# FFN gate and up of 18 tiles as seven half-size products per pair of tiles, with three low parts made by an adding DMA

## The chip, the cores and the metric

The kernel runs on one core of a Trainium2 chip. The metric is the device time in microseconds of one execution; three executions of the kernel before took 1146.77, 1148.54 and 1149.83 us (median 1148.54).

## The reference

One layer of a hybrid decoder is applied to 512 prompt tokens and 8 x 8 sample tokens, 576 columns in all, with D_MODEL = 1024 and D_FF = 2816, in float32. The mixer in front (three recurrent branches and `w_out`) is not touched. The part that is touched is the SwiGLU:

```python
hf = rmsnorm(x, p["norm_pre_ffn"][l])
f = (jax.nn.silu(hf @ p["ffn_w_gate"][l]) * (hf @ p["ffn_w_up"][l])) @ p["ffn_w_down"][l]
x = x + rmsnorm(f, p["norm_post_ffn"][l])
```

## The kernel before

Activations lie transposed: 128 rows of a feature tile on the partitions, 576 tokens along the row, treated as two halves of 288. D_MODEL is 8 such tiles (`KT`), D_FF is 22 (`FT`).

Each float32 operand is split into a high part in float32r and a low part, the rest. A product of 128x128 weights with 288 columns is then three matmuls: high by high, high by low, low by high (lines 202 to 204). Activations are split once (`split`, lines 239 and 240). Weights arrive as 512 KB (`raw`, 128 x 8 x 128) by a DMA that SyncE issues, and `wsplit` cuts each into two parts of 4 x 128 = 512 columns: ScalarE copies the high part (L184), VectorE subtracts for the low part (L185). Both stand under a high priority for the planner.

The order of the instructions on each engine is not written by hand. The framework plans it with a timeline simulation, by priority and readiness, and the engines then run their queues in that order, waiting on semaphores. `issue_after` (from `behind(marks, ...)`) holds chosen matmuls behind small norm matmuls.

The FFN begins after `w_out` and two norms (lines 1290 to 1310), which are worked half by half; `xr` holds the normed activations in float32 and `hf[k]` their high and low parts. FFN gate and up of the first four tiles (`NG`) run half by half, in the order `HB`, with their weights kept split in the pool `wq` (12 buffers of high and low) and, for tile 0, in `wp` (4 buffers). So half 0 of these tiles can cover the norm of half 1.

The other 18 tiles come in a loop: `mm3(ff_load(...), hf)` gives gate and up, 48 matmuls each, into PSUM (six banks); `glu` applies tanh and two VectorE steps per half; `act_split` splits the result into `fh` and `fl`. After every fourth tile `down` multiplies four finished tiles with `w_down` (8 output tiles x 2 halves x 12 matmuls, line 1374, `product`) and adds into `xr` (L1399; L1397 copies the first time). `down(FT - 6, 2)` and a last block of four tiles follow, then the final norm and the stores. Raw weights use four buffers, two in `wp` and two in `sx`; split weights of the loop use 16: three of four allocations go to `wq`, one to `wp`.

Of the kernel before, what the change touches and what calls it, by code (L numbers as in the profile page):

```python
# [8 lines left out]
F32 = mybir.dt.float32  # L9
# [3 lines left out]
OP = mybir.AluOpType  # L13
# [52 lines left out]
def hybrid_step(ctx: ExitStack, tc: tile.TileContext, i, o, dbg=None):  # L66
# [13 lines left out]
    def nm(s):  # L80
        cnt[0] += 1
        return f"{s}_{cnt[0]}"
# [93 lines left out]
    def wsplit(raw, alloc=None, eng=None):  # L176
        c = raw.shape[1]
        if alloc:
            hi, lo = alloc(c)
        else:  # L180
            hi = wp.tile([128, c, 128], F32R, name=nm("wh"), tag="wh")
            lo = wp.tile([128, c, 128], F32R, name=nm("wl"), tag="wl")
        with tc.high_priority(offset=HIPRI):
            S.activation(hi, raw, AF.Copy)  # L184
            (eng or lo_eng()).tensor_tensor(lo, raw, hi.bitcast(F32), op=OP.subtract)  # L185
        return hi, lo, c

    def mmp(name="mm"):
        return psm[0].tile([128, 512], F32, name=nm(name), tag="mm")[:, 0:NH]
# [17 lines left out]
    def behind(marks, pos, t, n=KT):  # L207
        out = {}
        for k in range(n):
            for ins, p in zip(marks, pos):  # L210
                if p <= t * n + k:
                    out[k] = ins
        return out

    def mm_half(ws, x, half, after=None):
        acc, k0 = mmp(), 0
        for w in ws:
            mm_part(acc, w, k0, len(x), x, half, after)
            k0 += w[2]
        return acc  # L220
# [49 lines left out]
    def hsl(half):  # L270
        return slice(NH * half, NH * half + NH)
# [998 lines left out]
    def two(pool, tag_h, tag_l, **kw):  # L1270
        return lambda c: (pool.tile([128, c, 128], F32R, name=nm("wh"), tag=tag_h, **kw),
                          pool.tile([128, c, 128], F32R, name=nm("wl"), tag=tag_l, **kw))
# [38 lines left out]
    mix.close()  # L1311


    tp2 = ctx.enter_context(tc.tile_pool(name="tp2", bufs=1, reuse_waits="tile"))
    ar = ctx.enter_context(tc.tile_pool(name="ar", bufs=4, reuse_waits="tile"))
    wq = ctx.enter_context(tc.tile_pool(name="wq", bufs=4 * NG - 4, reuse_waits="tile"))
    sx = ctx.enter_context(tc.tile_pool(name="sx", bufs=2, reuse_waits="tile"))
    fp = ctx.enter_context(tc.tile_pool(name="fp", bufs=7, reuse_waits="tile"))
    mx = xr
    acts, fs_ = {}, {}  # L1320

    def act(m):
        if m not in acts:
            acts[m] = ar.tile([128, NT], F32, name=nm("ar"), tag="ar")
        return acts[m]

    def glu(t, pg, pu):
        S.activation(t, pg, AF.Tanh, scale=0.5)
        V.scalar_tensor_tensor(t, t, 1.0, pg, op0=OP.add, op1=OP.mult)
        V.tensor_tensor(t, t, pu, op=OP.mult)  # L1330

    def act_split(m):
        fs_[m] = split(act(m), fp.tile([128, NT], F32R, name=nm("fh"), tag="fh"),
                       fp.tile([128, NT], F32R, name=nm("fl"), tag="fl"))

    wqn = [0]

    def ff_alloc(c):
        wqn[0] += 1
        return two(wq, "qh", "ql")(c) if wqn[0] % 4 else two(wp, "wh", "wl")(c)  # L1340

    rawn = [0]

    def ff_raw():
        rawn[0] += 1
        return (wp if rawn[0] % 2 else sx).tile([128, KT, 128], F32, name=nm("wr"), tag="wr", bufs=2)

    def ff_load(src, alloc=None):
        raw = ff_raw()
        SY.dma_start(raw, src)  # L1350
        return [wsplit(raw[:, a:a + KC, :], alloc or ff_alloc, eng=V) for a in range(0, KT, KC)]

    wg = []
    for m in range(NG):
        al = two(wq, "qh", "ql") if m else two(wp, "wh", "wl")
        wg.append([ff_load(i[w][m], al) for w in ("w_gate", "w_up")])
    for m in range(NG):
        act(m)
    for half in range(2):
        for j, m in enumerate(HB[half]):  # L1360
            glu(act(m)[:, hsl(half)],
                *[mm_half(w, hf, half, None if half else behind(marks, (11, 24, 54, 62), 2 * j + a))
                  for a, w in enumerate(wg[m])])
            if half:
                act_split(m)


    def down_w(m, k0, n):
# [1 line left out]
        SY.dma_start(raw.rearrange("p (m k) c -> p m k c", m=2),  # L1370
                     i["w_down"][m:m + 2, :, k0:k0 + n, :].rearrange("m p k c -> p m k c"))
        return raw

    def product(w, k0, x):
        hi, lo, _ = w
        acc = mmp()
        for k, (xh, xl) in enumerate(x):
            PE.matmul(acc, hi[:, k0 + k, :], xh, start=k == 0, stop=False)  # L1378
            PE.matmul(acc, hi[:, k0 + k, :], xl, start=False, stop=False)  # L1379
            PE.matmul(acc, lo[:, k0 + k, :], xh, start=False, stop=k == len(x) - 1)  # L1380
        return acc

    def down(k0, n):
        for m in range(0, KT, 2):
# [13 lines left out]
                    else:  # L1398
                        V.tensor_tensor(xv, xv, ps, op=OP.add)  # L1399

    for m in range(NG, FT):
        pg, pu = (mm3(ff_load(i[w][m]), hf) for w in ("w_gate", "w_up"))
        for half in range(2):
            glu(act(m)[:, hsl(half)], pg[half], pu[half])
        act_split(m)
        if m % 4 == 1 and m < FT - 1:
            down(m - 5, 4)
    down(FT - 6, 2)

    nl_w = [0]  # L1410
# [172 lines left out]
```

## Time and profile before

| | |
|---|---|
| Runs | 1146.77, 1148.54, 1149.83 us |
| Profiled execution | 1148.92 us, its span 1147.1 us |
| Mean granted TensorE clock | 0.973 of 2.4 GHz |
| Busy: PE, VectorE, ScalarE, GpSimd | 1072.0, 747.6, 405.2, 301.5 us |
| DMA | 98.60 MB, on the queue that SyncE feeds but for instruction fetches |
| FFN from the end of the norms to the last block | about 735 to 1117 us |

Times of the profile count from the first instruction of the span. PE is TensorE's matmul, PEld its weight load, DVE is VectorE, ACT is ScalarE, POOL is GpSimd, SP or SPq is SyncE's queue. A line "A <- B" in waits says that A stood idle until B released it. Matmuls overlap in the pipeline, so the mean duration of one is longer than the step from one to the next; the step is the time of a stretch divided by its matmuls.

### The profile page before, as it was taken

To read this page: it belongs to the slowest core of one execution; us is meant where nothing else is said; L and a number is where in the kernel's file an instruction comes from. 1 tells how busy PE (TensorE), PEld (TensorE's weight loads), DVE (VectorE), ACT (ScalarE), POOL (GpSimd) and SP (SyncE) were. 2 spreads that over 40 slices of the span, in tenths; PEclk is the share of its full clock that TensorE was granted. 3 is DMA by queue.
4 is the path that set the end of the run, shared out by engine and by line. 5 is a ranking of instruction groups with operands and counts; after the bars stand their busy time and mean duration, and the time that the engine had idled before them with its cause. 6 is when DMAs were issued, how large, how long until landed. Compare 5 with 4: busy or idle time off the path is not lost.

```text
span 1147.1 us, 20072 instructions
## 1 busy us (share of the span) xinstructions
PE 1072.0 (93%) x7874; PEld 1023.4 (89%) x7874; DVE 747.6 (65%) x1642; ACT 405.2 (35%) x807; POOL 301.5 (26%) x372
## 2 busy tenths in 40 slices
PE   6997887998988999999999898999999999999994
PEld 5896877988878988998899898999999999999994
DVE  8989999987897779744646658653344444443346
ACT  4255753334532442322333435343322322322210
POOL 6477664435462225221002332000000000000014
PEclk8999998998999999999999998999999999999997
DMA  5322213233223143312113613042222232213002
GB/s 193 109 86 71 78 43 90 70 100 117 88 63 103 48 134 101 81 51 102 56 52 101 214 66 134 22 154 83 86 81 84 82 87 80 89 59 93 1 2 83
DMA packets 61235, 98.60 MB, mean 86 GB/s; under 512 B 26059, under 2 KB 34387, under 8 KB 61139
## 3 DMA queue, kind: packets, MB, share of 16 engines
q1 hardware_dynamic: 61138, 97.31, 27.4%
q8 instruction: 62, 1.02, 0.4%
q14 instruction: 35, 0.28, 0.1%
HBM read 89.05 MB, written 8.24 MB: 85 GB/s over the span
## 4 chain that ended last, share of the span: by engine, by line
PE 66%; DVE 22%; DMA 4%; issue 3%; ACT 2%; POOL 2%; SPq 0%; DVEq 0%; ACTq 0%
PE mm L202 15%; PE mm L203 15%; PE mm L204 15%; PE mm L1380 4%; PE mm L1378 4%; PE mm L1379 4%; DVE wl L185 3%; DVE cv L423 2%; PE up L1182 1%; DVE bu L1052 1%; DMA bc<-in_s_bc 1%; PE rows L265 1%; PE zq L1164 1%; DVE h L377 1%; DVE brl L240 1%
## 5 line engine op out<-in xcount | busy, mean ns | idle before, releaser
L184 ACT ACTIVATE wh<-wr 128x512 fp32r<-128x512 f32 x268 | 166.2, 629 | 369.2 <-PE mm L203 221.4
L185 DVE TENSOR_TENSOR wl<-wr,wh 128x512 fp32r<-128x512 f32 x248 | 186.7, 758 | 161.4 <-ACT wh L184 154.0
L202 PE MATMUL mm<-hh,wh 128*128 128x288 f32 x768 | 236.4, 308 | 13.2 <-ACT pad L410 5.3
L204 PE MATMUL mm<-hh,wl 128*128 128x288 f32 x768 | 233.9, 305 | 0.0
L203 PE MATMUL mm<-hl,wh 128*128 128x288 f32 x768 | 233.8, 305 | 0.0
L203 PE MATMUL mm<-hfl,wh 128*128 128x288 f32 x704 | 208.1, 296 | 1.7 <-DVE hfl L240 1.7
L204 PE MATMUL mm<-hfh,wl 128*128 128x288 f32 x704 | 207.9, 296 | 0.0
L202 PE MATMUL mm<-hfh,wh 128*128 128x288 f32 x704 | 207.8, 296 | 0.0
L202 PEld LDWEIGHTS mm<-hh,wh 128*128 128x128 f32 x768 | 148.7, 194 | 20.4 <-issue 6.6
L203 PEld LDWEIGHTS mm<-hl,wh 128*128 128x128 f32 x768 | 148.5, 193 | 3.7 <-issue 3.1
L204 PEld LDWEIGHTS mm<-hh,wl 128*128 128x128 f32 x768 | 148.1, 193 | 2.2 <-issue 1.5
L203 PEld LDWEIGHTS mm<-hfl,wh 128*128 128x128 f32 x704 | 133.0, 189 | 2.0 <-DVE hfl L240 2.0
L202 PEld LDWEIGHTS mm<-hfh,wh 128*128 128x128 f32 x704 | 133.4, 190 | 0.0
L204 PEld LDWEIGHTS mm<-hfh,wl 128*128 128x128 f32 x704 | 133.2, 189 | 0.0
L1436 POOL TENSOR_TENSOR fs<-fs,fs 128x288 f32<-128x288 f32 x9 | 7.3, 807 | 399.3 <-ACT fs L1432 399.3
L1380 PE MATMUL mm<-fh,wl 128*128 128x288 f32 x352 | 103.9, 295 | 0.0
L1378 PE MATMUL mm<-fh,wh 128*128 128x288 f32 x320 | 94.4, 295 | 0.0
L1379 PE MATMUL mm<-fl,wh 128*128 128x288 f32 x320 | 94.3, 295 | 0.0
L202 PE MATMUL mm<-brh,wh 128*128 128x288 f32 x224 | 68.1, 305 | 8.5 <-DVE mg L801 5.9
L203 PE MATMUL mm<-brl,wh 128*128 128x288 f32 x224 | 67.9, 303 | 1.8 <-DVE brl L240 1.2
L204 PE MATMUL mm<-brh,wl 128*128 128x288 f32 x224 | 67.5, 302 | 0.0
L1380 PEld LDWEIGHTS mm<-fh,wl 128*128 128x128 f32 x352 | 66.1, 188 | 0.0
(477 smaller groups left out, 2055.9 us busy)
## 6 DMA issues: line engine op xcount, KB each, us to landing
wr<-in_w_in SPq DMA_DIRECT2D x48, 512.0 KB, 3.6
wr<-in_w_gate SPq DMA_DIRECT2D x22, 512.0 KB, 3.6
wr<-in_w_up SPq DMA_DIRECT2D x22, 512.0 KB, 3.6
wr<-in_w_down SPq DMA_DIRECT2D x20, 512.0 KB, 3.6
wr<-in_w_out SPq DMA_DIRECT2D x8, 512.0 KB, 3.6
xa<-in_x SPq DMA_DIRECT2D x8, 288.0 KB, 5.9
xr<-in_x SPq DMA_DIRECT2D x4, 576.0 KB, 7.4
out_y<-xr SPq DMA_DIRECT2D x16, 144.0 KB, 1.8
```

Source lines behind the costliest of these rows:

```text
L184: S.activation(hi, raw, AF.Copy)
L185: (eng or lo_eng()).tensor_tensor(lo, raw, hi.bitcast(F32), op=OP.subtract)
L202: PE.matmul(acc, hi[:, k, :], xh[:, sl], start=k0 + k == 0, stop=False)
L203: PE.matmul(acc, hi[:, k, :], xl[:, sl], start=False, stop=False)
L204: PE.matmul(acc, lo[:, k, :], xh[:, sl], start=False, stop=k0 + k == n - 1)
L240: V.tensor_tensor(lo, x, hi.bitcast(F32), op=OP.subtract)
L265: m0 = PE.matmul(rows[:, 96 * b:96 * b + 96], rc[:96, b:b + 1].to_broadcast([96, 128]), ident[:96, :96], start=True, stop=True).ins
L377: (G if half and k % 4 == 3 else V).tensor_tensor(t, xa[:, k, hsl(half)], rw_[half], op=OP.mult)
L423: V.scalar_tensor_tensor(y[:, :CW], pad[:, k:k + CW], w[k], y[:, :CW], op0=OP.mult, op1=OP.add)
L1378: PE.matmul(acc, hi[:, k0 + k, :], xh, start=k == 0, stop=False)
L1379: PE.matmul(acc, hi[:, k0 + k, :], xl, start=False, stop=False)
L1380: PE.matmul(acc, lo[:, k0 + k, :], xh, start=False, stop=k == len(x) - 1)
```

## The change

The 18 tiles are taken in nine pairs m, m + 1. For gate, and again for up, the 256 x 1024 weights of a pair and the 1024 x 576 activations are read as 2 x 2 blocks: weights a11, a12, a21, a22 of 128 x 512 (tile by half of the features), activations by half of the features and half of the tokens. The four blocks of the result are formed by Winograd's scheme of seven products instead of eight.

- `hf_sums` forms the activation side once, on VectorE, in place in `xr`: t1, t2, t3 and t4, four subtractions of 1152 columns. t1 and t2 are split into a new pool `st`, t3 into `sx`, t4 over `hf[0..3]` of half 1.
- `pair_w` loads both raw weights (two DMAs of 512 KB) and forms s1, a21, a11, a12 by four additions of 512 columns on VectorE. Four of the seven weights (w2, w3, w4, w5) are split as before by ScalarE and VectorE.
- `wsplit_dma` splits the other three, w0 = a11, w1 = a12, w6 = a22: ScalarE copies the high part, ScalarE writes its negative to the low part's buffer, and a DMA issued by GpSimd adds the raw weights from HBM onto that (256 KB each).
- `pair` runs the products in the order w0, w2, w3, w4, w1, w5, w6, 12 matmuls each. Three sums are formed in PSUM: w1 continues the bank of w0 (`px`), w5 that of w3 (`pz`), w6 that of w4 (`pw_`), after ScalarE or VectorE has read the bank. ScalarE copies px to u; VectorE makes u + w2's product, c22 = u + pz, c22 + pw, c12 = u + pz, c21 = u + pw.
- The GLU is cut into `glu_g`, applied when gate's block is done, and `glu_u`. Tile m is worked in halves, tile m + 1 in one piece of 576. `down` of four tiles now runs between gate and up of every second pair (m = 4, 8, 12, 16).
- Pools: the first four tiles use `wload`, with the two raw buffers of `wp`. `wq` is opened after `fp`, so its tiles lie elsewhere, and closed after the first four tiles; `sx` opens in its place. The seven-product loop and `down` have six buffers for split weights, four in `wp` and two in `sx`. `fp` has six buffers instead of seven, `ar` two of double size.

```diff
--- before.py
+++ after.py
@@ -1311,58 +1311,157 @@
     mix.close()
 
 
     tp2 = ctx.enter_context(tc.tile_pool(name="tp2", bufs=1, reuse_waits="tile"))
-    ar = ctx.enter_context(tc.tile_pool(name="ar", bufs=4, reuse_waits="tile"))
-    wq = ctx.enter_context(tc.tile_pool(name="wq", bufs=4 * NG - 4, reuse_waits="tile"))
-    sx = ctx.enter_context(tc.tile_pool(name="sx", bufs=2, reuse_waits="tile"))
-    fp = ctx.enter_context(tc.tile_pool(name="fp", bufs=7, reuse_waits="tile"))
-    mx = xr
+    ar = ctx.enter_context(tc.tile_pool(name="ar", bufs=2, reuse_waits="tile"))
+    fp = ctx.enter_context(tc.tile_pool(name="fp", bufs=6, reuse_waits="tile"))
+    st = ctx.enter_context(tc.tile_pool(name="st", bufs=1, side="right", reuse_waits="tile"))
+    wqx = ExitStack()
+    wq = wqx.enter_context(tc.tile_pool(name="wq", bufs=4 * NG - 4, reuse_waits="tile"))
     acts, fs_ = {}, {}
 
+    def hquad(a, b):
+        return [(hf[4 * a + k][0][:, hsl(b)], hf[4 * a + k][1][:, hsl(b)]) for k in range(4)]
+    def t_sums(b11, b12, b21, b22):
+        V.tensor_tensor(b11, b12, b11, op=OP.subtract)
+        V.tensor_tensor(b12, b22, b12, op=OP.subtract)
+        V.tensor_tensor(b22, b22, b11, op=OP.subtract)
+        V.tensor_tensor(b21, b21, b22, op=OP.subtract)
+    def parts(pool, src, tag):
+        c = src.shape[1]
+        hi, lo = (pool.tile([128, c, NH], F32R, name=nm(tag), tag=tag + e, bufs=1) for e in "hl")
+        split(src, hi, lo)
+        return [(hi[:, k, :], lo[:, k, :]) for k in range(c)]
+    def hf_sums():
+        b11, b12, b21, b22 = (xrt[:, 4 * a:4 * a + 4, hsl(b)] for a in range(2) for b in range(2))
+        t_sums(b11, b12, b21, b22)
+        return [hquad(0, 0), hquad(1, 0), parts(st, b22, "t2"), parts(st, b11, "t1"), b12, hquad(1, 1)]
+    def act2(m):
+        if m not in acts:
+            acts[m] = ar.tile([128, 2, NT], F32, name=nm("ar"), tag="ar")
+        return acts[m]
     def act(m):
-        if m not in acts:
-            acts[m] = ar.tile([128, NT], F32, name=nm("ar"), tag="ar")
-        return acts[m]
-    def glu(t, pg, pu):
+        return act2(m // 2 * 2)[:, m % 2, :]
+    def glu_g(t, pg):
         S.activation(t, pg, AF.Tanh, scale=0.5)
         V.scalar_tensor_tensor(t, t, 1.0, pg, op0=OP.add, op1=OP.mult)
+    def glu_u(t, pu):
         V.tensor_tensor(t, t, pu, op=OP.mult)
 
     def act_split(m):
         fs_[m] = split(act(m), fp.tile([128, NT], F32R, name=nm("fh"), tag="fh"),
                        fp.tile([128, NT], F32R, name=nm("fl"), tag="fl"))
 
-    wqn = [0]
-    def ff_alloc(c):
-        wqn[0] += 1
-        return two(wq, "qh", "ql")(c) if wqn[0] % 4 else two(wp, "wh", "wl")(c)
-    rawn = [0]
+    wg = []
+    for m in range(NG):
+        wg.append([wload(i[w][m], KT, two(wq, "qh", "ql") if m else None) for w in ("w_gate", "w_up")])
+    for m in range(NG):
+        act(m)
+    for half in range(2):
+        if half:
+            hx = hf_sums()
+        for j, m in enumerate(HB[half]):
+            pg, pu = (mm_half(w, hf, half, None if half else behind(marks, (11, 24, 54, 62), 2 * j + a))
+                      for a, w in enumerate(wg[m]))
+            glu_g(act(m)[:, hsl(half)], pg)
+            glu_u(act(m)[:, hsl(half)], pu)
+            if half:
+                act_split(m)
+    wqx.close()
+    sx = ctx.enter_context(tc.tile_pool(name="sx", bufs=2, reuse_waits="tile"))
+    hx[4] = parts(sx, hx[4], "t3")
+    t4 = hquad(0, 1)
+    for k in range(4):
+        split(xr[4 + k][:, hsl(0)], *t4[k])
+    hx.append(t4)
+    mx = xr
+    rawn, wqn = [0], [0]
 
     def ff_raw():
         rawn[0] += 1
         return (wp if rawn[0] % 2 else sx).tile([128, KT, 128], F32, name=nm("wr"), tag="wr", bufs=2)
 
-    def ff_load(src, alloc=None):
-        raw = ff_raw()
-        SY.dma_start(raw, src)
-        return [wsplit(raw[:, a:a + KC, :], alloc or ff_alloc, eng=V) for a in range(0, KT, KC)]
-    wg = []
-    for m in range(NG):
-        al = two(wq, "qh", "ql") if m else two(wp, "wh", "wl")
-        wg.append([ff_load(i[w][m], al) for w in ("w_gate", "w_up")])
-    for m in range(NG):
-        act(m)
-    for half in range(2):
-        for j, m in enumerate(HB[half]):
-            glu(act(m)[:, hsl(half)],
-                *[mm_half(w, hf, half, None if half else behind(marks, (11, 24, 54, 62), 2 * j + a))
-                  for a, w in enumerate(wg[m])])
-            if half:
-                act_split(m)
+    def ff_alloc(c):
+        wqn[0] += 1
+        return two(wp, "wh", "wl")(c) if wqn[0] % 3 else two(sx, "wh", "wl")(c)
+    def wsplit_dma(raw, src):
+        hi, lo = ff_alloc(KC)
+        with tc.high_priority(offset=HIPRI):
+            S.activation(hi, raw, AF.Copy)
+            S.activation(lo, hi.bitcast(F32), AF.Copy, scale=-1.0)
+            G.dma_start(lo, src, accum_op=OP.add)
+        return hi, lo, KC
+    def pair_w(src, m):
+        r = []
+        for a in range(2):
+            r.append(ff_raw())
+            SY.dma_start(r[a], src[m + a])
+        a11, a12, a21, a22 = (r[a][:, 4 * b:4 * b + 4, :] for a in range(2) for b in range(2))
+        d11, d12, d21, d22 = (src[m + a][:, 4 * b:4 * b + 4, :] for a in range(2) for b in range(2))
+        s1 = sx.tile([128, KC, 128], F32, name=nm("ws"), tag="ws")
+        with tc.high_priority(offset=HIPRI):
+            w0 = wsplit_dma(a11, d11)
+            V.tensor_tensor(s1, a21, a22, op=OP.add)
+            V.tensor_tensor(a21, a11, a21, op=OP.subtract)
+            V.tensor_tensor(a11, s1, a11, op=OP.subtract)
+            w2 = wsplit(a11, ff_alloc, eng=V)
+            w3 = wsplit(s1, ff_alloc, eng=V)
+            w4 = wsplit(a21, ff_alloc, eng=V)
+            w1 = wsplit_dma(a12, d12)
+            V.tensor_tensor(a12, a12, a11, op=OP.subtract)
+        return [w0, w1, w2, w3, w4, wsplit(a12, ff_alloc, eng=V), wsplit_dma(a22, d22)]
+    def product(w, k0, x, acc=None):
+        hi, lo, _ = w
+        new = acc is None
+        if new:
+            acc = mmp()
+        for k, (xh, xl) in enumerate(x):
+            PE.matmul(acc, hi[:, k0 + k, :], xh, start=new and k == 0, stop=False, skip_group_check=not new)
+            PE.matmul(acc, hi[:, k0 + k, :], xl, start=False, stop=False, skip_group_check=not new)
+            PE.matmul(acc, lo[:, k0 + k, :], xh, start=False, stop=k == len(x) - 1, skip_group_check=not new)
+        return acc
+    def pair(src, m, f):
+        ws = pair_w(src, m)
+        u = sx.tile([128, NH], F32, name=nm("cu"), tag="cu")
+        c12 = sx.tile([128, NH], F32, name=nm("c1"), tag="c1")
+        c2 = sx.tile([128, NT], F32, name=nm("c2"), tag="c2")
+        c21, c22 = c2[:, hsl(0)], c2[:, hsl(1)]
+        px = product(ws[0], 0, hx[0])
+        S.activation(u, px, AF.Copy)
+        V.tensor_tensor(u, u, product(ws[2], 0, hx[2]), op=OP.add)
+        pz = product(ws[3], 0, hx[3])
+        V.tensor_tensor(c22, u, pz, op=OP.add)
+        pw_ = product(ws[4], 0, hx[4])
+        V.tensor_tensor(c22, c22, pw_, op=OP.add)
+        product(ws[1], 0, hx[1], px)
+        f(0, hsl(0), px)
+        product(ws[5], 0, hx[5], pz)
+        V.tensor_tensor(c12, u, pz, op=OP.add)
+        f(0, hsl(1), c12)
+        product(ws[6], 0, hx[6], pw_)
+        V.tensor_tensor(c21, u, pw_, op=OP.add)
+        f(1, slice(0, NT), c2)
 
 
     def down_w(m, k0, n):
@@ -1370,15 +1469,6 @@
         SY.dma_start(raw.rearrange("p (m k) c -> p m k c", m=2),
                      i["w_down"][m:m + 2, :, k0:k0 + n, :].rearrange("m p k c -> p m k c"))
         return raw
-    def product(w, k0, x):
-        hi, lo, _ = w
-        acc = mmp()
-        for k, (xh, xl) in enumerate(x):
-            PE.matmul(acc, hi[:, k0 + k, :], xh, start=k == 0, stop=False)
-            PE.matmul(acc, hi[:, k0 + k, :], xl, start=False, stop=False)
-            PE.matmul(acc, lo[:, k0 + k, :], xh, start=False, stop=k == len(x) - 1)
-        return acc
 
     def down(k0, n):
         for m in range(0, KT, 2):
@@ -1398,13 +1488,14 @@
                     else:
                         V.tensor_tensor(xv, xv, ps, op=OP.add)
 
-    for m in range(NG, FT):
-        pg, pu = (mm3(ff_load(i[w][m]), hf) for w in ("w_gate", "w_up"))
-        for half in range(2):
-            glu(act(m)[:, hsl(half)], pg[half], pu[half])
+    for m in range(NG, FT, 2):
+        t = act2(m)
+        pair(i["w_gate"], m, lambda a, sl, c: glu_g(t[:, a, sl], c))
+        if m % 4 == 0 and m < FT - 2:
+            down(m - 4, 4)
+        pair(i["w_up"], m, lambda a, sl, c: glu_u(t[:, a, sl], c))
         act_split(m)
-        if m % 4 == 1 and m < FT - 1:
-            down(m - 5, 4)
+        act_split(m + 1)
     down(FT - 6, 2)
 
     nl_w = [0]
```

## Rows read from the trace of the kernel before

**Rows 1.** Page, parts 1 and 5: busy us, share; a group's count, busy, mean ns.

```profile
PE 1072.0 (93%) x7874; PEld 1023.4 (89%) x7874; DVE 747.6 (65%) x1642; ACT 405.2 (35%) x807; POOL 301.5 (26%) x372
...
L185 DVE TENSOR_TENSOR wl<-wr,wh 128x512 fp32r<-128x512 f32 x248 | 186.7, 758 | 161.4 <-ACT wh L184 154.0
```

**Rows 2.** By stretch: bounds, length, busy us (xcount) per engine, clock, DMA share, GB/s.

```profile
735.50:1100.00 364.50, 364.50 (x2754) 364.50 (x2753) 156.04 (x280) 105.34 (x193) 0.00 (x0) 1.00 0.26 79
...
785.00:810.00 25.00, 25.00 (x191) 25.00 (x190) 5.76 (x9) 10.75 (x24) 0.00 (x0) 1.00 0.29 85
...
705.00:710.00 5.00, 0.79 (x7) 0.59 (x5) 4.73 (x14) 2.68 (x6) 0.00 (x0) 0.88 0.76 249
710.00:715.00 5.00, 5.00 (x22) 5.00 (x23) 3.49 (x9) 1.33 (x3) 2.90 (x4) 0.50 0.49 188
```

**Rows 3.** Groups by line and shape, 770 to 1060 us: count, busy us, mean ns, idle.

```profile
L202 PE MATMUL mm<-hfh,wh 128*128 128x288 f32 x475 | 140.0, 295 | 0.0
...
L185 DVE TENSOR_TENSOR wl<-wr,wh 128x512 fp32r<-128x512 f32 x89 | 61.6, 692 | 100.1 <-ACT wh L184 94.9
L184 ACT ACTIVATE wh<-wr 128x512 fp32r<-128x512 f32 x89 | 56.3, 632 | 182.1 <-PE mm L203 82.5 <-PE mm L1379 68.1 <-issue 31.5
...
L1399 DVE TENSOR_TENSOR xr<-xr,mm 128x288 f32<-128x288 f32 x48 | 21.8, 454 | 33.0 <-PE mm L1380 33.0
...
L240 DVE TENSOR_TENSOR fl<-ar,fh 128x576 fp32r<-128x576 f32 x15 | 11.4, 758 | 0.0
```

**Rows 4.** Timelines of VectorE and ScalarE: start, length, instruction, idle before, releaser.

```profile
740.14 0.45 DVE L1329 SCALAR_TENSOR_TENSOR ar<-ar,mm 128x288 f32<-128x288 f32 x1
740.50 0.69 DVE L185 TENSOR_TENSOR wl<-wr,wh 128x512 fp32r<-128x512 f32 x1
...
758.94 2.50 DVE L185 TENSOR_TENSOR wl<-wr,wh 128x512 fp32r<-128x512 f32 x4 [0.38 <-ACT wh L184]
...
861.05 0.76 DVE L240 TENSOR_TENSOR fl<-ar,fh 128x576 fp32r<-128x576 f32 x1
861.73 0.45 DVE L1399 TENSOR_TENSOR xr<-xr,mm 128x288 f32<-128x288 f32 x1
...
889.06 0.69 DVE L185 TENSOR_TENSOR wl<-wr,wh 128x512 fp32r<-128x512 f32 x1 [2.47 <-ACT wh L184]
...
758.27 2.20 ACT L184 ACTIVATE wh<-wr 128x512 fp32r<-128x512 f32 x4 [2.55 <-DMA wr<-in_w_down]
...
866.13 0.63 ACT L184 ACTIVATE wh<-wr 128x512 fp32r<-128x512 f32 x1 [2.56 <-PE mm L1379]
```

**Rows 5.** Waits of PE, 600 to 1147 us: total us, times, longest.

```profile
PE rows L265 <- DVE rs_o L118: 6.7, 2, 4.2
...
PE mm L203 <- DVE hfl L240: 1.7, 1, 1.7
```

**Rows 6.** DMA queue; issues with KB and us to landing; weight loads 620 to 800.

```profile
q1 hardware_dynamic: 61138, 97.31, 27.4%
...
wr<-in_w_gate SPq DMA_DIRECT2D x22, 512.0 KB, 3.6
...
out_y<-xr SPq DMA_DIRECT2D x16, 144.0 KB, 1.8
...
wr<-in_w_down SPq DMA_DIRECT2D x4, 256.0 KB, 2.8
...
DMA to landing us min/median/max: 2.6/3.6/9.6
```

**Rows 7.** GpSimd's groups by line over the span.

```profile
L1287 POOL TENSOR_TENSOR sq<-sq,sq 128x288 f32<-128x288 f32 x12 | 10.1, 844 | 34.1 <-ACT sq L1284 34.1
...
L416 POOL COPY cst<-pad 128x24 f32<-128x24 f32 x16 | 4.5, 279 | 8.7 <-DVE pad L412 8.6
```

**Rows 8.** Chain of work that ended last: start, length, what.

```profile
700.04 4.06 DMA wr<-in_w_up
```

## The prediction, made before the result was known

> **What bounds the kernel now.** I read the page's busy times first: TensorE is busy 93% of the span, VectorE 65% [rows 1]. Such shares are averages over stages, so the table by stretch came next. From 735.5 to 1100 us, the FFN after its first four tiles' start, PE is busy 364.5 of 364.5 us at granted clock 1.00 with 2754 matmuls, which is 364.5 / 2754 = 0.1324 us each; VectorE is at 43%, ScalarE at 29%, GpSimd has no instruction there, and the DMA engines are 26% busy [rows 2]. (The 295 ns of one matmul in the list of groups overlaps its neighbours and is no cadence [rows 3].) Third, the waits of PE from 600 us on: no row names a weight split of the 18 tiles; what is there belongs to the norms, 6.7 us on the rsqrt chain of VectorE being the largest [rows 5]. So this stage is bound by the number of matmuls, and a matmul removed gives its cadence back, as long as everything that feeds PE keeps up. That condition is the whole question, since the change makes PE's work smaller and everybody else's larger.
>
> **What the change removes.** Before, gate and up of one tile take 8 x 3 x 2 = 48 matmuls each; two tiles of one weight ("pair" below) take 96. After, seven products of 4 x 3 = 12 matmuls: 84. There are 9 x 2 = 18 pairs, so 18 x 12 = 216 matmuls go, 216 x 0.1324 = **-28.6 us**. `down` keeps its 12 matmuls per product. One pair is now 84 x 0.1324 = 11.1 us, one product 1.59 us.
>
> **What it adds on VectorE.** Per pair: four sums of raw weights and four low parts, all 512 columns (before: eight low parts), five sums of results of 288 columns, then the GLU as 288 + 288 + 576 instead of four times 288; for up also two low parts of 576. Durations: 692 ns for 512, 454 for 288, 758 for 576 [rows 3]. That makes 8 x 0.692 + 5 x 0.454 + 0.45 + 0.45 + 0.76 = 9.5 us for gate and 11.0 for up, against 11.1 of PE: by these it would be a second bound. But consecutive instructions overlap: four of 512 stand in 2.50 us, so the step is (2.50 - 0.69) / 3 = 0.60; 288 to the next is 0.36 (740.14 to 740.50) and 576 to the next 0.68 (861.05 to 861.73) [rows 4]. By steps gate is 8 x 0.60 + 5 x 0.36 + 0.36 + 0.36 + 0.68 = 8.0 us, up 9.4, mean 8.7: 78% of PE's time. Every second pair has a `down` between (192 matmuls, 25.4 us of PE, 8 x 0.60 + 16 x 0.36 = 10.6 us of VectorE), which gives more room. I take VectorE as no bound.
>
> **ScalarE.** Ten copies of 512 per pair instead of eight, by step (2.20 - 0.63) / 3 = 0.52 [rows 4], one copy of 288, and the tanh or two high parts: 10 x 0.52 + 0.3 + 1.2 = 6.7 of 11.1 us. Hidden.
>
> **Waits inside a pair.** PE reopens three sums. Product w1 goes into px and must wait for ScalarE's copy of px, made after w0; three products lie between, 4.8 us. w5 into pz waits for VectorE's c22 = u + pz and w6 into pw for c22 += pw; two products lie between, 3.2 us, or five steps of 0.60. What is queued ahead in VectorE's order are low parts, which have priority and themselves wait for ScalarE and for a free buffer: the low part at 889.06 stood 2.47 us for its high part [rows 4]. A sum caught behind one costs PE about one step. Between nothing and all 36 sums by 0.6 us (21.6 us) I take a quarter, 9 x 0.6 = **+5.4 us**, nearer to nothing because the waits in the before trace fall in PE's own rhythm and never held it [rows 5].
>
> **The lookahead shrinks.** Split weights now live in six buffers (four in `wp`, two in `sx`) instead of sixteen, and a buffer serves 12 matmuls instead of 24. The before trace shows buffers being the limit for ScalarE already (each high part waits about 2.5 us for a matmul that frees one [rows 4]); PE does not notice with sixteen. After, a buffer is free when product n - 6 ends, and product n starts five products later: 5 x 1.59 = 7.9 us. An ordinary split needs 0.63 + 0.69 = 1.3 us of it. For w0, w1 and w6 the low part goes ScalarE copy, ScalarE negated copy (0.52 + 0.63 = 1.2 us), then an adding DMA from GpSimd. So 7.9 - 1.2 = **6.7 us** remain for GpSimd's issue, the transfer and its semaphore. All three weights of a pair are late by the same amount if one is, because a stall also delays the release of the next buffers: a transfer of L us costs L - 6.7 per pair, 18 (L - 6.7) in all, and no more.
>
> L is not in the trace: every data transfer is issued by SP on one queue [rows 6]. Nearest rows: a plain load of 256 KB lands in 2.8 us in this stage, one of 512 KB in 3.6; a store of 144 KB in 1.8; the slowest weight load after 620 us, with others queued, 9.6 [rows 6]. The adding transfer reads 256 KB from HBM and 256 KB of its destination, so I take 3.6, with GpSimd's issue as one of its 288-column operations, 0.84 [rows 7]: L = 4.4, hidden with 2.3 us to spare. Bounds: 1.8 + 0.28 [rows 7] = 2.1 us, no loss; 9.6 + 0.84 = 10.4, a loss of 18 x 3.7 = 67 us. The added traffic is 18 x 3 x 0.26 = 14 MB; the stage moves 79 GB/s x 364.5 us = 29 MB at 26%, so even counted twice it ends near 52%.
>
> The Trainium skill ("DMA: Bandwidth & Descriptors", section "Anatomy of one DMA — SWDGE (gpsimd) path") gives for a DMA issued by GpSimd 2.0 us plus the bytes at 436 GB/s, which would be an estimated 2.6 us here; no run here shows such a DMA, and by it nothing changes in the sum.
>
> **Getting into the first pair.** The four `wp` buffers are held by tile 0's gate and up, the last of the first stage; the first is free 36 matmuls, 4.8 us, before the boundary, and w0 needs 1.2 + 4.4 = 5.6: **+0.8 us**. The sums over hf: VectorE's slope (758 - 692) / 64 = 1.03 ns per column gives 1.35 us for 1152 columns; seven of those and four of 288 are 11.3 us, ScalarE about 5, beside 192 matmuls of half 1 (25.4 us) and the first products; t3 is needed 4.8 us into the pairs and t4 9.5. Cost nothing; without that cover VectorE's part of t3 and t4, 3.2 us.
>
> **The norms ahead of it.** The eight first weights now load through two buffers instead of four, and `wq` opens behind `fp`, over other tiles of the closed stage. Before, the last loads and splits come at 700 to 710 us, in front of half 1's rsqrt steps: one load waited for 4.06 us, PE stood 4.2 us in 705 to 710 and then had clock 0.50 in 710 to 715, 22 matmuls where 38 fit [rows 2, 8]. If the splits move earlier that is won, some 4.2 + 16 x 0.132 + 1.7 (the wait of hfl [rows 5]) = 8 us; but then 12 splits x 0.60 = 7 us stand in half 0's norm chain, which PE reaches with no slack. Between -8 and +7 I take 0.
>
> **Sum.** The profiled execution took 1148.9 us (span 1147.1 and 1.8 around it), 0.4 over the median of the runs. 1148.9 - 28.6 + 5.4 + 0.8 = 1126.5, less 0.4: **1126 us**.
>
> **Rivals.** (B) *VectorE sets the pace.* For: by durations up needs 11.0 of 11.1 us, and the queue is in order; where GpSimd works, the same split takes 758 ns on the page's mean against 692 here [rows 1, 3]. Against: the steps of 0.60. If about 1 us is lost per pair beyond the forecast's 0.3, 18 x 0.7 = 13 us more: 1139. (C) *The adding DMA is late: slower.* Its place is w6, w0 and w1 of each pair, its price 18 (L - 6.7), and with the other terms (-28.6 + 6.2 = -22) it decides from L = 6.7 + 22 / 18 = 7.9 us. For: loads that share the queues have taken 9.6, a raw pair of 1 MB is often in flight, and an addition is more than a copy. Against: the median of 3.6. At L = 9: 1126 + 41 = 1167; at 10.4: 1193. A stall of this kind may also cost clock: after the 4.2 us of idle time the granted clock stood at 0.50, the 1.2 GHz level [rows 2]. The Trainium skill ("TensorE: Matmul & The Clock Gate", section "HAM oscillation — how this bites in real kernels") says that a kernel whose bursts are each followed by a wait for data can fall to the half clock every time. The trace agrees at that one place. By it every pair at L = 10.4 would lose about another 2.1 us (22 matmuls for 38), 38 us in all, 1231. (D) *The norms gain as well:* 1126 - 8 = 1118, or less if no sum is late: 1113. (E) *The matmuls go but PE takes longer per product*, since each accumulation is only 12 long: `down` has the same 12, and from 785 to 810 us, nearly all `down`, PE does 191 matmuls in 25 us, 0.131 each [rows 2], so I give it no chance of its own.
>
> **How the numbers follow.** Forecast 0.47 (its own range 1119 to 1133); B 0.20, of it 0.03 within 0.3% of before; C 0.26, of it 0.04 within 0.3%; D 0.07. 0.3% (3.4 us) is about what a measurement tells from no change. Faster 0.47 + 0.17 + 0.07 = 0.71, same 0.07, slower 0.22. The range from 1112 to 1157 holds all of the forecast, B and D and the small third of C; what is left out is the long end of C, about 0.17.
>
> **What would show it.** Right: some 216 matmuls fewer, PE near 100% at clock 1.00 in the pairs, adding transfers landing in under 6.5 us, VectorE near 80% there. Wrong: PE waiting for GpSimd's queue at w6, w0 or w1 with high parts on time (C); PE waiting for c22 or u (B); other idle time at 696 to 735 us than before.

## The result, and the profile after

The changed kernel takes 1132.93 us (median of its runs, 1131.65 to 1140.19), the kernel before on the same chip 1147.65: ratio 0.9883, 95% interval 0.9837 to 0.9928. That is 1.2% faster, inside the range of 1112 to 1157, and 7 us over the forecast of 1126. The profiled execution took 1131.71 us, its span is 1129.9, against 1147.1 before.

First the page of the kernel after, against [rows 1, 6]: the engines' busy times, the two data queues (packets, MB, share of the 16 engines' span), and the weight loads and adding transfers with their median us from issue to landing.

```profile
PE 1048.5 (93%) x7658; PEld 997.0 (88%) x7658; DVE 829.2 (73%) x1797; ACT 476.9 (42%) x931; POOL 348.1 (31%) x426
...
q1 hardware_dynamic: 61138, 97.31, 27.5%
q0 software_dynamic: 7776, 14.16, 7.8%
...
wr<-in_w_gate SPq DMA_DIRECT2D x22, 512.0 KB, 3.5
wr<-in_w_up SPq DMA_DIRECT2D x22, 512.0 KB, 4.5
wr<-in_w_down SPq DMA_DIRECT2D x20, 512.0 KB, 5.3
...
wl<-in_w_gate POOLq DMA_DIRECT2D x27, 256.0 KB, 5.1
wl<-in_w_up POOLq DMA_DIRECT2D x27, 256.0 KB, 4.5
```

216 matmuls are gone (7874 - 7658). The 54 adding transfers have a queue of their own, and their 14.16 MB take 7.8% of the engines' time, where 97.31 MB of plain loads take 27.5%: about twice as much per MB. The raw loads of two of the weights got slower too: 4.5 us for w_up and 5.3 for w_down, where each took 3.6 before.

Then the table by stretch, against [rows 2], columns as there:

```profile
705.00:710.00 5.00, 4.76 (x36) 4.53 (x35) 3.93 (x14) 2.51 (x5) 0.00 (x0) 1.00 0.58 179
710.00:715.00 5.00, 4.31 (x33) 4.34 (x34) 4.09 (x12) 3.03 (x7) 2.06 (x3) 1.00 0.41 135
730.00:735.00 5.00, 2.90 (x13) 2.49 (x14) 5.00 (x12) 3.08 (x8) 0.00 (x0) 0.86 0.00 0
735.00:740.00 5.00, 5.00 (x33) 5.00 (x32) 5.00 (x9) 1.16 (x1) 0.00 (x0) 0.80 0.02 3
...
760.00:1060.00 300.00, 293.54 (x2200) 292.04 (x2200) 203.80 (x373) 156.07 (x282) 44.00 (x51) 1.00 0.55 132
```

In 760 to 1060 PE is no longer busy all the time: 6.5 us are missing, and 2200 matmuls stand where 300 / 0.1324 = 2266 would fit. VectorE is at 68%, the DMA engines at 55%. In the norms the hole at 705 to 710 is filled. From 730 to 740 PE now does 13 and 33 matmuls, with the clock at 0.86 and 0.80; the kernel before did 25 and 40 there, at 1.00:

```profile
730.00:735.00 5.00, 3.26 (x25) 3.02 (x24) 5.00 (x14) 3.03 (x8) 0.00 (x0) 1.00 0.00 0
735.00:740.00 5.00, 5.00 (x40) 5.00 (x39) 2.03 (x5) 1.77 (x4) 0.00 (x0) 1.00 0.01 3
```

What PE waits for, from 600 to 1130 us, against [rows 5] (total us, times, longest):

```profile
PE mm L1440 <- DMA wl<-in_w_up: 4.3, 4, 1.8
PE rows L265 <- DVE rs_o L118: 3.4, 2, 2.5
...
PE mm L1440 <- DMA wl<-in_w_gate: 2.2, 2, 1.5
PE mm L202 <- DVE ar L1364: 1.9, 1, 1.9
```

All waits that the profile lists in the pairs are for adding transfers: six at L1440, the matmul that reads a low part, 6.5 us in all. No row names one of the sums that PE reopens. One of the six in the chain of waits (start, length, what), from issue to the matmul:

```profile
823.76 7.10 DMA wl<-in_w_up
830.86 0.04 issue
830.91 0.40 PE mm L1440
```

And the 54 adding transfers by tile (time on GpSimd in ns, then landing):

```profile
L1409 POOL DMA_DIRECT2D wl<-in_w_gate x27: 856/862/1202, 756.6 to 1052.6; - x27
L1409 POOL DMA_DIRECT2D wl<-in_w_up x27: 856/862/865, 783.2 to 1063.1; - x27
...
DMA to landing us min/median/max: 4.0/4.9/7.4
```

The median of 4.9, issue included, against the forecast's 4.4, mixes two kinds. Sorted by what the timelines show in flight when a transfer is issued, the 20 with no raw load in flight landed in 4.0 to 4.7 us (median 4.1); the 34 with one or two in flight took 4.1 to 7.4 (median 6.1). In the order of issue (w0, w1, w6 of each pair), 17 of the 18 for w1 are of the first kind; w0 and w6 have medians of 6.0 and 6.1. Of the six waits four are w6's, two are w0's, the entry's among them, and none is w1's.

Of the six that PE waited for, four were issued 1 to 3 us after raw loads (the one at 823.76 follows w_down loads issued from 822.30 on). One came behind a raw load that was itself late (6.2 us), and then took 7.4 us itself beside another raw load; one is the entry's. In 820 to 832 us, the strip shows the share of the DMA engines' time in 40 slices, in tenths: from 823 to 831 us they are mostly 80% busy or more, and the adding queue takes more of their time than the raw loads do, with fewer MB (0.79 against 1.05):

```profile
DMA  0000000007669999899988997996999999985210
...
q0 software_dynamic: 432, 0.79, 40.4%
q1 hardware_dynamic: 544, 1.05, 27.2%
```

For the experiments one measure is used beside the time: the length of the 18 tiles' stage, from its first to its last matmul of gate and up, less its matmuls at 0.1325 us each. What is left is PE's idle time in the stage, and what a lower clock costs there; in the table it is called idle.

| kernel | time, us | ratio to before, 95% interval | stage, us | matmuls | idle, us |
|---|---|---|---|---|---|
| before | 1147.65 beside the first run of after, 1149.4 to 1150.3 beside the others | | 330.7 | 2496 | -0.1 |
| less216 | 1120.71 | 0.9745 [0.9726, 0.9764] | 302.1 | 2280 | 0.0 |
| front_only | 1146.41 | 0.9978 [0.9961, 0.9994] | 330.7 | 2496 | -0.1 |
| after, first run | 1132.93 | 0.9883 [0.9837, 0.9928] | 310.9 | 2280 | 8.8 |
| again | 1131.94 | 0.9846 [0.9816, 0.9877] | 310.3 | 2280 | 8.2 |
| no_add | 1121.07 | 0.9762 [0.9738, 0.9786] | 302.6 | 2280 | 0.5 |
| seven_buf | 1128.57 | 0.9825 [0.9798, 0.9853] | 306.8 | 2280 | 4.7 |
| all_v | 1122.89 | 0.9784 [0.9755, 0.9812] | 307.0 | 2292 | 3.3 |
| all_v_seven | 1123.49 | 0.9774 [0.9753, 0.9796] | 303.8 | 2283 | 1.3 |
| spare_neg | 1120.17 | 0.9739 [0.9716, 0.9762] | 306.7 | 2291 | 3.1 |
| spare_load | 1127.91 | 0.9812 [0.9798, 0.9827] | 308.8 | 2292 | 5.1 |
| spare_add | 1132.30 | 0.9854 [0.9834, 0.9875] | 313.6 | 2292 | 9.9 |
| one_add | 1131.81 | 0.9838 [0.9822, 0.9855] | 312.7 | 2285 | 10.0 |

(A few matmuls of `down` stand inside the stage in the last rows; the count takes them in.) The time also holds what the stage doesn't: ahead of the FFN the source is the same in all, and yet the first matmul over hf came at 693.4 to 702.4 us in these executions, and not quite alike in one and the same kernel (699.5 in the first profile after, 700.7 in the second). So a time's median is read with its interval, and a stall by the stage.

### The profile page after: what moved, and what is told of

Its sections match the earlier page's. It is cut to its first block, busy times and chain, and to the rows that moved or that the text cites. A ratio compares the mean times of both kernels' runs of the same rounds, so it can differ in the third digit from the quotient of the medians.

```text
span 1129.9 us, 20130 instructions
## 1 busy us (share of the span) xinstructions
PE 1048.5 (93%) x7658; PEld 997.0 (88%) x7658; DVE 829.2 (73%) x1797; ACT 476.9 (42%) x931; POOL 348.1 (31%) x426
## 3 DMA queue, kind: packets, MB, share of 16 engines
q1 hardware_dynamic: 61138, 97.31, 27.5%
q0 software_dynamic: 7776, 14.16, 7.8%
## 4 chain that ended last, share of the span: by engine, by line
PE 56%; DVE 25%; DMA 8%; issue 5%; POOL 3%; ACT 2%; SPq 0%; DVEq 0%; POOLq 0%; ACTq 0%
PE mm L1440 8%; PE mm L1438 8%; PE mm L1439 8%; PE mm L203 8%; PE mm L202 8%; PE mm L204 7%; DVE wl L185 4%; DMA wl<-in_w_up 2%; DVE cv L423 2%; DMA eg<-bgd 1%; DMA bc<-in_s_bc 1%; PE up L1182 1%; ACT wh L184 1%; DVE h L377 1%; DMA wr<-in_w_gate 1%
## 5 line engine op out<-in xcount | busy, mean ns | idle before, releaser
L184 ACT ACTIVATE wh<-wr 128x512 fp32r<-128x512 f32 x250 | 155.2, 629 | 233.0 <-PE mm L203 110.9
L185 DVE TENSOR_TENSOR wl<-wr,wh 128x512 fp32r<-128x512 f32 x230 | 174.5, 764 | 72.8 <-ACT wh L184 68.8
L1440 PE MATMUL mm<-fh,wl 128*128 128x288 f32 x352 | 103.5, 295 | 0.0
L1440 PE MATMUL mm<-hfh,wl 128*128 128x288 f32 x288 | 83.9, 297 | 6.5 <-DMA wl<-in_w_up 4.3
L1438 PE MATMUL mm<-hfh,wh 128*128 128x288 f32 x288 | 84.6, 295 | 0.0
L1439 PE MATMUL mm<-hfl,wh 128*128 128x288 f32 x288 | 84.5, 294 | 0.0
L1409 POOL DMA_DIRECT2D wl<-in_w_up x27 | 23.3, 862 | 179.7 <-ACT wl L1408 89.4
L1440 PEld LDWEIGHTS mm<-fh,wl 128*128 128x128 f32 x352 | 66.0, 188 | 0.0
L803 POOL TENSOR_TENSOR mg<-mg,mt 128x576 f32<-128x576 f32 x16 | 28.2, 1760 | 120.2 <-DVE mt L801 90.7
L1439 PE MATMUL mm<-t,wh 128*128 128x288 f32 x216 | 64.0, 296 | 0.0
L1438 PE MATMUL mm<-t,wh 128*128 128x288 f32 x216 | 63.7, 295 | 0.0
```

The costliest lines, as they stand in the source:

```text
L803: G.tensor_tensor(acc[m], acc[m], dst[:, :NT], op=OP.add)
L1409: G.dma_start(lo, src, accum_op=OP.add)
L1438: PE.matmul(acc, hi[:, k0 + k, :], xh, start=new and k == 0, stop=False, skip_group_check=not new)
```

## The experiments

The theory (A in the expectations): the adding transfers are late where raw loads are in flight on the same engines, and PE waits for them. The rivals: chance, or GpSimd's issue (B); VectorE's order, masked by the transfers (C, the prediction's rival B); and the traffic itself, whoever waits for its data.

**Is it the same again?** `again` is the changed kernel, unchanged.

> The changed kernel once more, unchanged, for its own spread and a second trace. Theory A (adding transfers come late where raw loads of 1 MB or more are in flight on the same DMA engines): 1131 to 1135 us, PE waits 5 to 8 us on the adding transfers, at the same few products as in the first trace (those whose transfer is issued 1 to 3 us after two or more raw loads). Theory B (the lateness is chance, or comes from GpSimd's issue): the same sum at other products.

1131.94 us. The six waits came at the same products, 0.4 to 1.1 us later in the span each, and sum to 5.7 us:

```profile
PE mm L1440 <- DMA wl<-in_w_up: 4.0, 4, 1.6
PE mm L1440 <- DMA wl<-in_w_gate: 1.7, 2, 1.0
```

They belong to the plan of the kernel, not to chance.

**The price of the matmuls.** `less216` is the kernel before with as many matmuls left out, 12 of the 48 of each second tile's product:

```
-    def mm3(ws, x):
+    def mm3(ws, x, short=False):
...
+                if short and half and k0:
+                    continue
...
-        pg, pu = (mm3(ff_load(i[w][m]), hf) for w in ("w_gate", "w_up"))
+        pg, pu = (mm3(ff_load(i[w][m]), hf, m % 2 == 1) for w in ("w_gate", "w_up"))
```

> The kernel before with 216 matmuls of gate and up left out (12 of the 48 of each second tile's product: its second half gets only four of eight weight blocks, so the result is not the reference's), nothing else changed: the price of the removed matmuls alone. By the forecast's first term 216 x 0.1324 = 28.6 us, so the 18 tiles take 302.1 us instead of 330.7 and the time is 1149.65 - 28.6 = 1121 us. If the 18 tiles are bound by something beside PE's count once PE is shorter (VectorE, loads), less comes: over 1125.

1120.71 us, 28.7 less than the kernel before beside it (1149.38), and the stage is 330.7 - 302.1 = 28.6 shorter with no idle time. The forecast's first term, 28.6, is the price of these matmuls to a tenth.

**The front.** `front_only` is the kernel before with the pools and the first eight weights of the change:

```
+    fp = ctx.enter_context(tc.tile_pool(name="fp", bufs=6, reuse_waits="tile"))
...
-    fp = ctx.enter_context(tc.tile_pool(name="fp", bufs=7, reuse_waits="tile"))
...
-        al = two(wq, "qh", "ql") if m else two(wp, "wh", "wl")
-        wg.append([ff_load(i[w][m], al) for w in ("w_gate", "w_up")])
+        wg.append([wload(i[w][m], KT, two(wq, "qh", "ql") if m else None) for w in ("w_gate", "w_up")])
```

> The kernel before with only the front of the change: fp with six buffers opened ahead of wq, and the first eight weights loaded through two raw buffers; the 18 tiles as before. The forecast put the norms at 0 between -8 and +7 us. From the profiles, the norms' stage of the changed kernel took 60.2 us against 62.5 before: if that is the front's doing, -2.3 us, about 1147.4. If it is the spread of executions, 1149.65 and no difference in the stage's length.

1146.41 us: 3.0 less than the kernel before beside it (by the interval 0.7 to 4.5). The stretch from the first matmul over hf to the pairs is 59.7 us (699.40 to 759.09) where it was 62.5 (695.44 to 757.91). Waits of PE from 690 to 765 us, then two stretches, of this kernel:

```profile
PE mm L202 <- DVE ar L1330: 1.9, 1, 1.9
PE rows L265 <- DVE rs_o L118: 0.8, 1, 0.8
```

```profile
705.00:710.00 5.00, 4.67 (x36) 4.43 (x34) 4.08 (x15) 2.60 (x5) 0.00 (x0) 1.00 0.58 177
...
730.00:735.00 5.00, 3.06 (x14) 2.75 (x14) 5.00 (x14) 2.66 (x7) 0.00 (x0) 0.75 0.00 0
```

The same picture as in the changed kernel: the wait of 4.2 us and its half clock are gone [rows 2, 5], and the moved splits now stand in VectorE's order further on (7.0 us busy from 720 to 730, 4.7 before), where PE waits 1.9 us for it and loses clock at 730 to 735.

**What the adding DMA costs.** `no_add` leaves the 54 transfers out; the three low parts then hold the negated high part alone:

```
-            G.dma_start(lo, src, accum_op=OP.add)
```

> The adding DMA is left out (the low parts of w0, w1, w6 then hold only the negated high part, so the output is not the reference's); ScalarE's two copies stay. Theory A: PE's waits on the adding transfers, 6.5 us in the first trace, go, and raw loads land in 3.6 us again: 1124 to 1127. Theory C (VectorE's order is what holds PE, the transfers only mask it): within 2 us of the changed kernel, with waits of PE on VectorE in place of those on the DMA.

1121.07 us, 10.9 less than `again` beside it; the stage has 0.5 us idle where it had 8.2. The time is below what was expected (1124 to 1127 us). VectorE and ScalarE still have all their instructions, and PE is busy throughout:

```profile
760.00:1060.00 300.00, 300.00 (x2264) 300.00 (x2263) 211.40 (x384) 161.43 (x289) 0.00 (x0) 1.00 0.29 94
```

So VectorE's order (theory C) and rival B hold nothing up; the DMA is the whole loss in the stage. Raw loads of w_up land in 3.6 us again, those of w_down in 4.2 (5.3 with the transfers), so a part of their lateness is this kernel's own.

**More time for it.** `seven_buf` gives the split weights a seventh buffer:

```
-        return two(wp, "wh", "wl")(c) if wqn[0] % 3 else two(sx, "wh", "wl")(c)
+        return two(wp, "wh", "wl")(c) if wqn[0] % 7 in (1, 2, 4, 6) else two(sx, "wh", "wl", bufs=3)(c)
```

> A seventh buffer for split weights (four in wp, three in sx, allocated 4 to 3). A buffer then comes free six products ahead instead of five: 8.3 us instead of 6.7 remain for issue and transfer. Theory A: the longest landing was 7.1 us and its issue waits little, so all lateness of the loop goes: 1126 to 1128, the wait at the first pair (0.7 us) may stay. Theory C: within 2 us of the changed kernel.

1128.57 us. The idle time falls to 4.7, but not all lateness of the loop goes, though that was expected: a transfer still took up to 8.0 us, and four waits for adding transfers are left, the entry's among them:

```profile
PE mm L1440 <- DMA wl<-in_w_gate: 1.9, 3, 1.0
PE mm L1440 <- DMA wl<-in_w_up: 0.6, 1, 0.6
```

**None of it.** `all_v` makes the three low parts on VectorE:

```
-            S.activation(lo, hi.bitcast(F32), AF.Copy, scale=-1.0)
-            G.dma_start(lo, src, accum_op=OP.add)
+            V.tensor_tensor(lo, raw, hi.bitcast(F32), op=OP.subtract)
```

> The three low parts of each pair on VectorE (one subtraction each) in place of ScalarE's negated copy and the adding DMA. VectorE then has 8.7 + 3 x 0.60 = 10.5 us of 11.1 per pair by steps. Theory A with VectorE near its limit: PE waits on VectorE appear, 0.5 us per pair or more, 1134 to 1150. Theory D (VectorE's steps still fit and the DMA was not needed): no waits on either, 1124 to 1127.

1122.89 us, better than both kernels and than either theory said. VectorE has 232 us of 300, and PE still waits only on entering the pairs (1.6 us, for a high part of ScalarE) and 0.4 us once, for VectorE:

```profile
760.00:1060.00 300.00, 299.54 (x2255) 298.88 (x2254) 232.08 (x433) 127.31 (x233) 0.00 (x0) 1.00 0.29 91
```

`all_v_seven` is both edits together.

> The three low parts by VectorE instead of the adding DMA, and seven split buffers instead of six (four in wp, three in sx). If the remaining steps of the stage with low parts by VectorE (1.6 us at ScalarE's high part on entering the first pair, 0.4 us at a low part, some 2.6 us of small steps) come from the buffers, the entry's 1.6 us goes and the time is about 1121 us. If they are VectorE's own order, nothing changes: 1122.9. If VectorE, 77% busy there, is in the way once buffers come free earlier and low parts pass the sums, the stage grows and the time is over 1125.

1123.49 us. The entry's wait fell to 0.5 us and the idle time to 1.3, so that wait was for a buffer, but the time can't be told from `all_v`.

**Late at the product, or costly by its traffic?** `spare_add` is `all_v` with the copy and the transfer into a buffer that nobody reads, so that no product can wait for it (the first line stands in `all_v` too):

```
             V.tensor_tensor(lo, raw, hi.bitcast(F32), op=OP.subtract)
+            sc = sx.tile([128, KC, 128], F32R, name=nm("sc"), tag="sc", bufs=3)
+            S.activation(sc, hi.bitcast(F32), AF.Copy, scale=-1.0)
+            G.dma_start(sc, src, accum_op=OP.add)
```

> Low parts by VectorE, and beside them ScalarE's negated copy and GpSimd's adding transfer, as in the changed kernel, into a spare buffer that nobody reads: the same 14 MB and the same issues, but no product waits for them. Theory A (the adding transfer is late at a product): the pairs take what they take with VectorE's low parts, 307.0 us, and the time is 1120 to 1124 us. Rival (the transfers cost by their traffic, by making raw loads late): PE waits for high parts of late raw loads, some 5 us or more, and the time is 1127 or more; the raw loads land later than the 3.6 us of the kernel before.

1132.30 us, where theory A had 1120 to 1124: the rival's time came. Here is its longest stall in the chain of waits:

```profile
1033.71 5.98 DMA wr<-in_w_up
1039.69 0.02 issue
1039.72 0.04 DVE ws L1424
1039.75 0.57 issue
1040.33 0.75 DVE ar L1361
1041.08 0.38 DVE c L1456
1041.45 0.04 issue
1041.50 0.40 PE mm L1440
```

A raw load is late, VectorE's first sum over it (ws) stands for it, and behind it in VectorE's order the sum c, which PE needs before it can reopen the bank: 3.1 us of PE. After it PE ran near half clock for some 3 us. So the forecast's stall at a reopened sum does exist, in this kernel, but behind a load, not behind a split. `spare_neg` leaves only the transfer out of it, `spare_load` makes it a plain load:

```
-            G.dma_start(sc, src, accum_op=OP.add)
+            G.dma_start(sc, src.bitcast(F32R))
```

> The kernel with the spare buffer without its 54 adding transfers: low parts by VectorE, and ScalarE's negated copy into a buffer that nobody reads. Theory (the transfers' traffic made the spare kernel 9.4 us slower than low parts by VectorE alone): 1121 to 1125 us, raw loads of up back at about 4.1 us. Rival (the 54 more copies in ScalarE's order hold high parts back): 1130 to 1133.

> The kernel with the spare buffer with plain loads of the same 256 KB from GpSimd's queue in place of the adding ones: same issues, same bytes from HBM, no addition. If what costs is the time that adding takes of the DMA engines (6.2 against 3.2 us of 16 engines per MB), about half of the 9.4 us goes or more: 1123 to 1128. If it is the 54 issues or the bytes, nothing goes: 1130 to 1134.

1120.17 and 1127.91 us. ScalarE's 54 copies cost nothing. A plain load costs part of what the adding one does: idle 3.1, 5.1 and 9.9 us; 7.7 of the 12.1 us between the medians of `spare_neg` and `spare_add`. VectorE's waits for raw loads at ws rise with it (count, busy, mean ns, idle before and its releasers; `spare_neg`, `spare_load`, `spare_add`):

```profile
L1423 DVE TENSOR_TENSOR ws<-wr 128x512 f32<-128x512 f32 x18 | 12.5, 692 | 16.9 <-DMA wr<-in_w_up 12.3 <-DMA wr<-in_w_gate 4.4
```

```profile
L1424 DVE TENSOR_TENSOR ws<-wr 128x512 f32<-128x512 f32 x18 | 12.5, 692 | 29.6 <-DMA wr<-in_w_up 20.6 <-DMA wr<-in_w_gate 9.1
```

```profile
L1424 DVE TENSOR_TENSOR ws<-wr 128x512 f32<-128x512 f32 x18 | 12.5, 692 | 41.8 <-DMA wr<-in_w_up 26.2 <-DMA wr<-in_w_gate 15.6
```

The profiled execution of `spare_load` was its fastest run (1121.0 of 1121.0 to 1131.1), so its 7.7 us over `spare_neg` are not all seen in that trace; where the other runs lost theirs stays open.

The framework plans each kernel's order anew. In the stage VectorE's order is the same in `spare_load` and `spare_add`, so the 4.4 us between their medians are the price of adding over loading. `spare_neg` has another order in places: at the stall above it has the next VectorE step (0.66 us) in front of ws, not behind it. What the new order has of the 7.7 us between `spare_neg` and `spare_load` was not tested.

**One of the three.** `one_add` keeps the transfer for w6 and takes w0 and w1 to VectorE:

```
-    def wsplit_dma(raw, src):
+    def wsplit_dma(raw, src, add=False):
+        if not add:
+            return wsplit(raw, ff_alloc, eng=V)
...
-        return [w0, w1, w2, w3, w4, wsplit(a12, ff_alloc, eng=V), wsplit_dma(a22, d22)]
+        return [w0, w1, w2, w3, w4, wsplit(a12, ff_alloc, eng=V), wsplit_dma(a22, d22, True)]
```

> The changed kernel with the adding transfer for w6 alone, 18 instead of 54; w0's and w1's low parts by VectorE. If each adding transfer costs alike, a third of the 9.0 us between the changed kernel (1131.9) and the one with all low parts by VectorE (1122.9) is left: 1125.9. If they hurt only where three of a pair meet raw loads, 1122 to 1124; if w6 at the end of the pair is the one that is late, over 1128.

1131.81 us: a third of the transfers, and all of the loss, as was expected if w6 is the one that is late. Waits of PE from 740 to 1075 us, and the landing of the 18:

```profile
PE mm L1442 <- DMA wl<-in_w_up: 3.1, 4, 1.2
PE mm L1442 <- DMA wl<-in_w_gate: 2.6, 4, 1.2
PE mm L1440 <- ACT wh L184: 1.6, 1, 1.6
```

```profile
DMA to landing us min/median/max: 4.2/5.8/7.1
```

w6 is late in 8 of 18 pairs, with no other adding transfer in flight beside any of the 18. All 18 were issued with one or two raw loads in flight, and w6 takes nearly what it took in the kernel after (median 5.8 against 6.1). So the other adding transfers aren't needed to make it late, and raw loads are what is left; that they do it was not tried by moving them. The wait for ScalarE (1.6 us) is the entry's, as in `all_v`. VectorE has two more low parts per pair here and another order, so that w6 alone costs as much as all three did isn't shown to hold in the changed kernel's order.

## Why the prediction was right or wrong

- **The removed matmuls, -28.6: right.** `less216` gave -28.7 in time and -28.6 in the stage.
- **The reopened sums, +5.4: wrong.** No wait of PE names one in the kernel after, and with the transfers away the whole stage has 0.5 us idle. A sum behind a low part costs PE nothing here. That the total came near the forecast is partly luck: this term stood where the next one was missing.
- **The adding DMA, "hidden with 2.3 us to spare": wrong, and the main error.** It costs 8 us in the stage, 10.9 by the medians. What failed first is that L was one number, 4.4, the same for every transfer: it is 4.1 (median) with no raw load in flight at the issue and 6.1 with one or two, up to 7.4. And then the step from it: "All three weights of a pair are late by the same amount", 18 (L - 6.7). By that formula 4.1 and 6.1 both cost nothing, and the maximum of 7.4 would cost 12.6. In the trace six of 54 are late, none of them w1's, and in `one_add` w6 alone is late in 8 of 18 pairs. The budget was also too long: the transfer issued at 823.76 took 7.10 and PE lost 1.49 us (its matmul came at 830.91, the one before it at 829.29, and a step is 0.13), so 5.6 from issue were free there. Rival C named the mechanism and its place, but for w1, and its bound of 7.9 for the break-even was not reached.
- **"Even counted twice it ends near 52%": the share was right (55%), its cost of nothing was not.** A mean share hides the stretches where raw loads and adding transfers are in flight together; in `spare_add` such traffic, with nobody waiting for its data, goes with 9.9 us idle against 3.1 in `spare_neg`, an unknown part of it from the other order. There VectorE has the three low parts too; in the changed kernel no wait of PE names a raw load or a sum.
- **The entry, +0.8: right.** The first of the six waits is 0.7 us, for w0, and ended at 760.79.
- **The norms, 0: off by 3.0 us.** The part that was to be won was won: the wait of 4.2 us and the half clock behind it are gone. With 8 us put on it, the 3.0 that came would mean that 5 were given back; the rows name where (splits in VectorE's order, PE's wait of 1.9 us, clock), but these 5 us were not measured by themselves.
- **VectorE no bound: right.** Even with the three low parts added, at 77% (232.08 / 300), PE waits for it 0.4 us (`all_v`). Rival B fell; the 0.60 steps were the right reading, not the durations.
- **The sum.** -28.7 (`less216`) - 3.0 (`front_only`) + 10.9 (`no_add` to `again`) = -20.8; `again` stood 17.7 below before. Of the remaining 3.1 the stage of `no_add` shows 0.5; the rest is not located, and is no more than the intervals of these terms leave.

## What to carry to other kernels

Price a transfer by its landings beside the loads that it will meet, not by a median over all, price what it does to those loads, and look at the DMA share of the 10 us around it instead of the stage's mean. Work moved to the DMA engines was not free where loads shared them: here VectorE had 32% idle time, and giving it the 54 low parts (1122.9 us) beats handing them to DMA (1131.9). Where VectorE's order had an instruction on a raw load in front of a sum that TensorE needed, a late load stalled TensorE through that sum (3.1 us in `spare_add`).

## What the runs showed of the hardware

- The adding transfer of 256 KB takes the engines longer than a plain load of the same bytes from the same queue: 7.6% of 1129.0 us x 16 engines for 14.16 MB (`spare_add`) against 4.5% of 1119.2 (`spare_load`), 1.7 times. The queue's rows of the two pages, in that order:

```profile
q0 software_dynamic: 7776, 14.16, 7.6%
```

```profile
q0 software_dynamic: 7776, 14.16, 4.5%
```

- It landed in 3.9 / 5.4 / 7.6 us (minimum, median, maximum; `spare_add`), the plain one in 2.8 / 4.3 / 6.0. The Trainium skill ("DMA: Bandwidth & Descriptors", section "Anatomy of one DMA — SWDGE (gpsimd) path") would give an estimated 2.6 us; that is near the fastest plain load, and no adding one came near it.
- An adding transfer lands later when plain loads of 512 KB are in flight at its issue: in the kernel after a median of 4.1 us with none (20 transfers), 6.1 with one or two (34).
- GpSimd is busy 0.86 us for each adding issue.
- A stall of 3.1 us in the pairs cost clock, the longest of 1.8 us in the kernel after did not. After the wait that ended at 1041.50 (`spare_add`) the granted clock was near its 1.2 GHz level; after the one of 1.8 us in the kernel after, that ended at 976.1, it stayed at 1.00. In the norms of the kernel after one of nearly that length did cost clock: a stall of 1.9 us that ended at 733.0, with one of 0.3 us ahead of it and five matmuls between, was followed by a clock of 0.80 from 735 to 740. Each kernel's stretch after its stall in the pairs:

```profile
1041.50:1045.00 3.50, 3.50 (x14) 3.19 (x15) 3.18 (x7) 0.75 (x2) 0.00 (x0) 0.54 0.68 182
```

```profile
976.00:979.00 3.00, 2.88 (x21) 2.88 (x22) 1.25 (x3) 0.63 (x1) 0.37 (x1) 1.00 0.69 110
```
